# Scaled weights kept in DRAM, a growing lead in the output projection, and another order of z around attention

## The chip, the cores and the metric

The kernel runs on one core of one Trainium2 chip. The metric is the device time of one execution in microseconds (us), smaller is better. TensorE is called PE here, VectorE DVE, ScalarE ACT, GpSimd POOL, and SyncE, which only issues DMAs in this kernel, SP.

## The reference

A decoder trunk of two layers works on 1024 tokens of width 1024 in float32. Layer 0 is a gated MLP with a spatial mixing in chunks of 128 tokens, then one shared pair of keys and values is made, and layer 1 is sliding-window attention:

```python
u, v, z = split(rms_norm(h, a_pre) @ w_in, 3)            # 2048 wide each
v = layer_norm(gelu(v), ln_g, ln_b)
s = einsum('gts,bnsgc->bntgc', tril(w_s), chunks(v)) + b_s
h = h + rms_norm((gelu(u) * s * silu(z)) @ w_out, a_post)
k, v = rms_norm(h, kv_norm) @ w_k, rms_norm(h, kv_norm) @ w_v   # shared, 4 heads of 64
q, z = split(rms_norm(h, b_pre) @ b_in, 2)               # 1024 wide each
o = attention(q, k, v)          # 16 heads, window 128, ALiBi, sinks
h = h + rms_norm((o * silu(z)) @ b_out, b_post)
```

## The kernel before, in words

**Products.** The kernel keeps float32 accuracy by splitting every operand into a high part (made by ACT, L105) and a low part (made by DVE, L106), and by taking three matmuls for one product (`mm3`, L168 to L170): high by high, high by low, low by high. Nearly all of PE's time goes into these, in shapes of 128x128 by 128x512. The large products of layer 0 use a recursive scheme that multiplies sums of blocks.

**Halves.** The 1024 tokens are two halves of 512 (h = 0, 1). Activations of a half stand transposed, eight pieces of 128 rows by 512 tokens.

**Layer 0.** The v projection begins with its first step written out by hand (L400 to L420): x and the weights r0 are loaded in pieces of 512 columns, ACT scales x, DVE casts the weights (L411) and makes both low parts (L412, L414). After u, z and the spatial mixing, the gated products are stored to DRAM as `td`, seven sets m = 1 to 7 by eight groups. Four sets of each group are differences made by POOL (`sums`, L616, by the helper line L205) and stored by SP one after the other (L617).

**Output projection** (`out_layer`, L761). Its 28 steps (m, u) each need a piece of `td` (`t_prep`, loaded by SP into `oraw` P2a, then split) and a piece of weights, mostly a sum of two loaded blocks (`s_sum`, loaded into `oraw` P2b and other places, then split by `s_prep`). `prep(n)` prepares step n and makes the sum of step n + 3 (`LEAD = 3`); the sums of steps 0 to 2 stand ahead of the first `prep`. The order in which these are written sets the order of SP's loads.

**Layer 1.** `Weights` (L112) hands out the weight tiles of layer 1, 128x1024 float32 each, in a fixed order: q and kv and z of the first half, then kv, q and z of the second. SP loads a tile two ahead into one of three buffers (`raw_w`). For a q or z tile POOL multiplies its eight blocks of 128 columns by eight gains, one for each partition and block (L140, eight instructions), in both halves anew. Then ACT and DVE split it. A q or z tile is used in eight products of three matmuls, 24 in all, and handed to the queue in four parts, called steps here. The k and v weights take 16 steps for a half, and are split with the gain in the split itself (L109, L110).

**Attention** runs in units, 16 for each half. A unit makes its scores (L1015, L1021) for four heads, DVE and ACT turn them into probabilities, PE transposes these (L1050) into `pt`, ACT copies them (`pc`, L1053), POOL masks the copy in place (L1054), DVE masks another copy (`pp`, L1057), and PE takes eight values matmuls (`o`, L1068 and L1071). `attn` writes the scores of unit i, the values of unit i - 2 and the transposes of unit i - 1 together, and behind them as many filling steps as the schedule gives: `total` steps are spread over 36 places in attention 0, over 30 in attention 1.

**Order.** At the bottom (L1168 to L1196) stands the schedule: the q phase of half 0 beside the residual sum of layer 0 (`chain_a`, which squares and sums rows on ACT, L182, and takes the reciprocal root on POOL, L178), then kv, then z tiles and attention. Each engine has its own queue in program order; a scheduler places the instructions into it. ACT's queue also takes DMA issues.

Of the kernel before, what the change touches and what calls it, by code (L numbers as in the profile page):

```python
# [14 lines left out]
P = 128  # L15
# [35 lines left out]
def tile_yoco(  # L51
# [56 lines left out]
    def split_scaled(hi, lo, src, g):  # L108
        nc.scalar.activation(hi, src, AF.Copy, scale=g)  # L109
        nc.vector.scalar_tensor_tensor(lo, src, g, hi.bitcast(F32), ALU.mult, ALU.subtract)  # L110

    class Weights:  # L112


        def __init__(self):
            self.order = []
            q, z = ([(wqz[i, m], "q") for m in range(8)] for i in range(2))
            kv = [(wkv[kp], f"kv{kp}") for kp in range(4)]
            self.order += q + kv + z + kv + q + z
            self.order += [(wo_b[gd, cp], "") for gd in range(2) for cp in range(4)]  # L120
            self.raw, self.done, self.at = [], [], 0

        def load(self, i):
            while len(self.raw) <= min(i, len(self.order) - 1):
                n = len(self.raw)
                src, kind = self.order[n]
                self.raw.append(wload(src, f"w{n}"))

        def split(self, i):
            while len(self.done) <= min(i, len(self.order) - 1):  # L130
                n = len(self.done)
                self.load(n)
                raw, kind = self.raw[n], self.order[n][1]
                hi = wpool.tile([P, 1024], F32R, tag="whi", name=f"whi{n}")
                lo = wpool.tile([P, 1024], F32R, tag="wlo", name=f"wlo{n}")
                halves = [slice(kk * 512, kk * 512 + 512) for kk in range(2)]
                if kind == "q":
                    rv = raw.rearrange("p (k c) -> p k c", k=KT)
                    for k in range(KT):
                        nc.gpsimd.tensor_scalar(rv[:, k], rv[:, k], gain(G_BPRE, k), None, ALU.mult)  # L140
                if kind[:2] == "kv":
                    for kk, cs in enumerate(halves):
                        split_scaled(hi[:, cs], lo[:, cs], raw[:, cs], gain(G_KV, 2 * int(kind[2:]) + kk))
                else:
                    split(hi, lo, raw)
                self.done.append((hi, lo))

# [140 lines left out]
    def v_layer(ahead):  # L288
# [119 lines left out]
        for k in range(2):  # L408
            cs = slice(k * 512, k * 512 + 512)
            nc.scalar.activation(T[1][0][:, k], xa[:, 0, k], AF.Copy, scale=g(0, k))  # L410
            nc.vector.tensor_copy(p0[0][:, cs], r0[:, cs])  # L411
            nc.vector.scalar_tensor_tensor(T[1][1][:, k], xa[:, 0, k], g(0, k), T[1][0][:, k].bitcast(F32),  # L412
# [348 lines left out]
    def out_layer():  # L761
# [61 lines left out]

        def prep(n):
            if n < len(steps):
                ready[n] = (t_prep(*steps[n]), s_prep(*steps[n]))
            if n + LEAD < len(steps):
                s_sum(*steps[n + LEAD])

        LEAD = 3  # L830
        yo = [None, None]
# [361 lines left out]

    fill = chain(z_phase(1, n1, z1, 2, 8), tail())
    attn(1, q1, z1, fill, 56, 2)
    drain(fill)  # L1196
# [61 lines left out]
```

## Time and profile before

| what | value |
|---|---|
| runs | 1062.0, 1063.74, 1064.31 us (median 1063.74) |
| profiled execution, its own time | 1062.32 us |
| its span | 1060.6 us, 14401 instructions |
| granted clock of PE | 0.999 |
| DVE, ACT, POOL busy | 71%, 55%, 34% |
| DMA | 159.76 MB, mean 151 GB/s; HBM read 127.37 MB, written 31.46 MB |

The span is what the profile shows from the first to the last instruction; the execution's own time has some 1.7 us around it. A row of the timeline gives the start, the duration of one or a run of instructions, the engine, the line of the program, the operation and its operands, and in brackets how long the engine was idle before it and what ended that. Matmuls are pipelined, so the step from one start to the next is what a matmul costs, not its printed duration. The list of waits gives total, number and longest in us.

### The profile page before, as it was taken

How to read it: one execution, taken by the hardware profiler on the slowest of the kernel's cores; microseconds unless marked ns; L12 is line 12 of the kernel's file. 1: busy time of each engine (PE TensorE's matmuls, PEld its weight loads, DVE VectorE, ACT ScalarE, POOL GpSimd, SP SyncE). 2: the span in 40 equal slices, each digit the busy share in tenths (PEclk: the TensorE clock that was granted, in tenths of full speed). 3: DMA queues.
4: the chain of work that ended last, by engine and by line, in shares of the span. 5: the costliest groups of instructions: out<-in, count | busy, mean ns of one | idle time of the engine just before them, and what ended most of it. 6: DMA issues, size and time to landing. Idle time of an engine off the chain costs nothing.

```text
span 1060.6 us, 14401 instructions
## 1 busy us (share of the span) xinstructions
PE 1045.6 (99%) x5114; PEld 856.6 (81%) x5114; DVE 757.9 (71%) x1353; ACT 581.3 (55%) x981; POOL 357.2 (34%) x407
## 2 busy tenths in 40 slices
PE   9999999999999999999999999999999999999997
PEld 7887788888888888888788888888778778777776
DVE  7987466867767768668696686655767874777873
ACT  6684454555564555464444564545785555765631
POOL 0000003254253442540100354648617779400120
PEclk9999999999999999999999999999999999999999
DMA  8787252434333423348987533734211212112353
GB/s 314 264 284 255 97 180 89 133 110 135 115 109 125 143 105 130 115 142 285 337 304 268 195 140 95 258 100 145 94 60 61 80 60 80 60 60 80 120 179 119
DMA packets 68710, 159.76 MB, mean 151 GB/s; under 512 B 6176, under 2 KB 16800, under 8 KB 68640
## 3 DMA queue, kind: packets, MB, share of 16 engines
q1 hardware_dynamic: 63600, 150.11, 41.7%
q10 hardware_dynamic: 5040, 8.75, 2.3%
q8 instruction: 40, 0.66, 0.3%
q14 instruction: 30, 0.25, 0.1%
HBM read 127.37 MB, written 31.46 MB: 150 GB/s over the span
## 4 chain that ended last, share of the span: by engine, by line
PE 83%; DVE 5%; issue 5%; POOL 3%; DMA 2%; ACT 1%; SPq 0%; DVEq 0%; POOLq 0%; ACTq 0%
PE ob L168 5%; PE ob L170 5%; PE ob L169 5%; PE ub L168 5%; PE ub L170 5%; PE ub L169 5%; PE qz L168 5%; PE qz L169 5%; PE qz L170 5%; PE uc L168 2%; PE uc L170 2%; PE uc L169 2%; PE sp L596 2%; PE vb L169 2%; PE vb L170 2%
## 5 line engine op out<-in xcount | busy, mean ns | idle before, releaser
L140 POOL TENSOR_SCALAR raw_w<-raw_w,gn 128x128 f32<-128x128 f32 x256 | 183.8, 736 | 160.0 <-DVE ohiloP0b L106 93.5
L168 PE MATMUL qz<-n_hi,whi 128*128 128x512 f32 x256 | 102.2, 399 | 0.1
L170 PE MATMUL qz<-n_hi,wlo 128*128 128x512 f32 x256 | 100.2, 391 | 0.0
L169 PE MATMUL qz<-n_lo,whi 128*128 128x512 f32 x256 | 100.0, 390 | 0.0
L106 DVE TENSOR_TENSOR wlo<-raw_w,whi 128x1024 fp32r<-128x1024 f32 x40 | 49.5, 1238 | 37.7 <-ACT whi L105 34.7
L1054 POOL TENSOR_SCALAR_AFFINE_SELECT pc<-pc 128x512 f32<-128x512 f32 x32 | 25.3, 791 | 119.2 <-ACT pc L1053 119.2
L105 ACT ACTIVATE whi<-raw_w 128x1024 fp32r<-128x1024 f32 x40 | 42.2, 1055 | 40.6 <-PE qz L169 14.2
L205 POOL TENSOR_TENSOR f<-raw_uz 128x512 f32<-128x512 f32 x15 | 19.4, 1291 | 130.0 <-DMA bsb<-in_bs_dram 85.7
L205 POOL TENSOR_TENSOR f<-raw_uz,raw_uz 128x512 f32<-128x512 f32 x15 | 19.2, 1280 | 124.9 <-DVE uzhilo_g L106 124.9
L105 ACT ACTIVATE uzhilo_g<-f 128x1024 fp32r<-128x1024 f32 x31 | 32.9, 1060 | 47.7 <-PE uc L170 42.5
L170 PEld LDWEIGHTS qz<-n_hi,wlo 128*128 128x128 f32 x256 | 48.1, 188 | 10.8 <-DVE wlo L106 0.6
L168 PEld LDWEIGHTS qz<-n_hi,whi 128*128 128x128 f32 x256 | 48.1, 188 | 10.7 <-ACT whi L105 0.4
L169 PEld LDWEIGHTS qz<-n_lo,whi 128*128 128x128 f32 x256 | 48.2, 188 | 9.3
L208 ACT ACTIVATE uz_slots<-ub 128x512 f32<-128x512 f32 x48 | 28.4, 591 | 43.6 <-PE ub L170 41.3
L106 DVE TENSOR_TENSOR uzhilo_g<-f,uzhilo_g 128x1024 fp32r<-128x1024 f32 x31 | 39.0, 1257 | 18.6 <-ACT uzhilo_g L105 18.6
L1037 ACT ACTIVATE pr<-pr,nm 128x129 f32<-128x129 f32 x128 | 49.8, 391 | 3.9 <-DVE nm L1035 3.8
L168 PE MATMUL ub<-T,whi_g 128*128 128x512 f32 x128 | 50.6, 396 | 0.0
L168 PE MATMUL ub<-T,uzhilo_g 128*128 128x512 f32 x128 | 50.5, 394 | 0.0
L170 PE MATMUL ub<-T,wlo_g 128*128 128x512 f32 x128 | 49.9, 390 | 0.0
L170 PE MATMUL ub<-T,uzhilo_g 128*128 128x512 f32 x128 | 49.9, 390 | 0.0
L169 PE MATMUL ub<-T,whi_g 128*128 128x512 f32 x128 | 49.8, 389 | 0.0
L169 PE MATMUL ub<-T,uzhilo_g 128*128 128x512 f32 x128 | 49.8, 389 | 0.0
(328 smaller groups left out, 3225.3 us busy)
## 6 DMA issues: line engine op xcount, KB each, us to landing
raw_uz<-in_wuz_in_dram SPq DMA_DIRECT2D x32, 512.0 KB, 3.5
raw_w<-in_wqz_dram SPq DMA_DIRECT2D x32, 512.0 KB, 3.5
td<-uz_slots SPq DMA_DIRECT2D x56, 256.0 KB, 2.2
orawP2a<-td SPq DMA_DIRECT2D x28, 512.0 KB, 4.1
raw<-in_wv_in_dram SPq DMA_DIRECT2D x17, 512.0 KB, 5.3
vg<-vd SPq DMA_DIRECT2D x8, 1024.0 KB, 5.4
orawP2b<-in_wo_a_dram SPq DMA_DIRECT2D x16, 512.0 KB, 5.8
vraw<-in_wv_in_dram SPq DMA_DIRECT2D x13, 512.0 KB, 4.7
```

Of the source, the lines that this page charges most:

```text
L105: nc.scalar.activation(hi, src, AF.Copy)
L106: nc.vector.tensor_tensor(lo, src, hi.bitcast(F32), ALU.subtract)
L140: nc.gpsimd.tensor_scalar(rv[:, k], rv[:, k], gain(G_BPRE, k), None, ALU.mult)
L168: nc.tensor.matmul(out, lhsT=a_hi, rhs=b_hi, start=start, stop=False, skip_group_check=True)
L169: nc.tensor.matmul(out, lhsT=a_hi, rhs=b_lo, start=False, stop=False, skip_group_check=True)
L170: nc.tensor.matmul(out, lhsT=a_lo, rhs=b_hi, start=False, stop=stop, skip_group_check=True)
L205: (eng or nc.vector).tensor_tensor(out, a, b, op)
L208: nc.scalar.activation(out, a, AF.Copy)
L596: nc.tensor.matmul(psv[:, n], lhsT=d["vg"][:, 4 * j + n, i * P:(i + 1) * P], rhs=d["wc"], start=True, stop=True)
L1037: nc.scalar.activation(pr[:, i], pr[:, i], AF.Exp, bias=nm[:, i // 2, i % 2:i % 2 + 1], accum_out=dn[:, i // 2, i % 2:i % 2 + 1])
L1054: nc.gpsimd.affine_select(pc, pc, [[0, 4], [1, P]], ALU.is_ge, 0.0, base=0, channel_multiplier=-1)
```

## The change

There are four edits.

1. *Weights.* A q or z tile of the first half is multiplied by one POOL instruction over 128x1024, with the gains broadcast along each block, in place of eight. The scaled tile is then stored to a DRAM tile `wsc` by a DMA that ACT issues (16 stores of 512 KB). The second half loads `wsc`, and POOL scales nothing there.
2. *First v step.* The two casts of r0 (128x512) go from DVE to POOL.
3. *Output projection.* Ahead of `prep(n)` sums are made up to step n + min(3, max(0, n - 4) // 2), so the lead grows from 0 to 3; `prep(0)` and `prep(1)` both stand ahead of the loads of `s_view`.
4. *Schedule.* All eight z tiles of half 0, with the norm of half 1 beside them, precede attention 0. It is filled with kv, q and the first four z tiles of half 1, 64 steps (72 of 80 before, and two z tiles of half 1 alone behind it). Attention 1 is filled with the other four z tiles and the tail, 48 steps (56 before).

```diff
+    wsc = [[dram.tile([P, 1024], F32, name=f"wsc{i}_{m}") for m in range(8)] for i in range(2)]
...
-            q, z = ([(wqz[i, m], "q") for m in range(8)] for i in range(2))
-            kv = [(wkv[kp], f"kv{kp}") for kp in range(4)]
-            self.order += q + kv + z + kv + q + z
+            q, z = ([(wqz[i, m], "q", wsc[i][m]) for m in range(8)] for i in range(2))
+            q1, z1 = ([(wsc[i][m], "", None) for m in range(8)] for i in range(2))
+            kv = [(wkv[kp], f"kv{kp}", None) for kp in range(4)]
+            self.order += q + kv + z + kv + q1 + z1
...
                 if kind == "q":
                     rv = raw.rearrange("p (k c) -> p k c", k=KT)
-                    for k in range(KT):
-                        nc.gpsimd.tensor_scalar(rv[:, k], rv[:, k], gain(G_BPRE, k), None, ALU.mult)
+                    g = gn[:, G_BPRE:G_BPRE + KT].unsqueeze(2).broadcast_to([P, KT, P])
+                    nc.gpsimd.tensor_tensor(rv, rv, g, ALU.mult)
...
                     split(hi, lo, raw)
+                if back is not None:
+                    nc.scalar.dma_start(out=back, in_=raw)
...
-            nc.vector.tensor_copy(p0[0][:, cs], r0[:, cs])
+            nc.gpsimd.tensor_copy(p0[0][:, cs], r0[:, cs])
...
         def prep(n):
+
+            while sums[0] < len(steps) and sums[0] <= n + min(3, max(0, n - 4) // 2):
+                s_sum(*steps[sums[0]])
+                sums[0] += 1
             if n < len(steps):
                 ready[n] = (t_prep(*steps[n]), s_prep(*steps[n]))
-            if n + LEAD < len(steps):
-                s_sum(*steps[n + LEAD])
-
-        LEAD = 3
+
+        sums = [0]
...
-        for n in range(2):
-            s_sum(*steps[n])
-        s_sum(*steps[2])
         prep(0)
+        prep(1)
         for u in range(4):
             fetch(s_view(u), u, 1, 0)
-        prep(1)
...
-    for _ in z_phase(0, n0, z0, 0, 2):
+    for _ in z_phase(0, n0, z0, 0, 8):
         step(side)
+    drain(side)
     q1 = pair("P3", "q1")
-    fill = chain(z_phase(0, n0, z0, 2, 8), side, kv_phase(1, n1), q_phase(1, n1, q1))
-    attn(0, q0, z0, fill, 72)
+    fill = chain(kv_phase(1, n1), q_phase(1, n1, q1), z_phase(1, n1, z1, 0, 4))
+    attn(0, q0, z0, fill, 64)
     drain(fill)
-    drain(z_phase(1, n1, z1, 0, 2))
...
-    fill = chain(z_phase(1, n1, z1, 2, 8), tail())
-    attn(1, q1, z1, fill, 56, 2)
+    fill = chain(z_phase(1, n1, z1, 4, 8), tail())
+    attn(1, q1, z1, fill, 48, 2)
```

Lines of the changed kernel are five or six higher than those of the one before. Three places show how the queues move.

SP's queue at the start of the output projection, before. `td4` to `td7` are stores of POOL's differences, `orawP2a` takes pieces of `td`, `orawP2b` pieces of weights, `gpa` is a gain:

```order
L710 DMA gpa_3835<-in_a_post_dram 128x1024
L236 DMA orawP2b_3841<-in_wo_a_dram 128x2x512
L617 DMA td5_99<-uz_slots_1333 128x512
L617 DMA td6_100<-uz_slots_1333 128x512
L617 DMA td7_101<-uz_slots4_1334 128x512
L617 DMA td4_98<-uz_slots_1333 128x512
L236 DMA orawP2b_3841<-in_wo_a_dram 128x2x512
L236 DMA orawP2a_3840<-td1_95 128x2x512
L236 DMA scho_3837<-in_wo_a_dram 128x2x512 x4
```

The same place in the changed kernel:

```order
L716 DMA gpa_3851<-in_a_post_dram 128x1024
L242 DMA orawP2a_3856<-td1_111 128x2x512
L623 DMA td5_115<-uz_slots_1349 128x512
L623 DMA td6_116<-uz_slots_1349 128x512
L623 DMA td7_117<-uz_slots4_1350 128x512
L623 DMA td4_114<-uz_slots_1349 128x512
L242 DMA orawP2b_3857<-in_wo_a_dram 128x2x512 x2
L242 DMA scho_3853<-in_wo_a_dram 128x2x512 x4
```

The load of `td1` moved from behind the four stores to ahead of them, and one load of weights moved behind them.

ACT's queue at the end of layer 0 (`junk_oa01` are the last sums of squares of the projection, `n0` the normed half 0, `whi` the high parts of q tiles), before:

```order
L105 ACTIVATE whi1_4989<-raw_w1_4857 128x1024
L105 ACTIVATE n0_hi_4588<-nt0_3_0_4913 128x4x128
L105 ACTIVATE n0_hi_4588<-nt0_3_1_4920 128x4x128
L182 ACTIVATE junk_oa01_0_4940,ssa1_3843<-yoa1_2_4289 128x512
L182 ACTIVATE junk_oa01_1_4944,ssa1_3843<-yoa1_2_4289 128x512
L182 ACTIVATE junk_oa01_2_4948,ssa1_3843<-yoa1_3_4290 128x512
L182 ACTIVATE junk_oa01_3_4952,ssa1_3843<-yoa1_3_4290 128x512
L105 ACTIVATE whi2_5049<-raw_w2_4859 128x1024
```

And in the changed kernel:

```order
L105 ACTIVATE whi1_4999<-raw_w1_4873 128x1024
L151 DMA wsc0_3_91<-raw_w3_5005 128x1024
L105 ACTIVATE n0_hi_4604<-nt0_3_0_4929 128x4x128
L105 ACTIVATE n0_hi_4604<-nt0_3_1_4936 128x4x128
L188 ACTIVATE junk_oa01_0_4956,ssa1_3859<-yoa1_2_4305 128x512
L151 DMA wsc0_4_92<-raw_w4_5059 128x1024
L188 ACTIVATE junk_oa01_1_4960,ssa1_3859<-yoa1_2_4305 128x512
L188 ACTIVATE junk_oa01_2_4964,ssa1_3859<-yoa1_3_4306 128x512
L188 ACTIVATE junk_oa01_3_4968,ssa1_3859<-yoa1_3_4306 128x512
L105 ACTIVATE whi2_5053<-raw_w2_4875 128x1024
```

Two stores of scaled tiles now stand among them; each waits for POOL's multiply of its tile.

PE's queue in attention 0, the values of unit 0_1 (`o_0_1`), the transposes (`pt_0_1`) and the filling matmuls behind them, before:

```order
L1068 MATMUL o_0_1_6412<-pc_0_1_6335,vt 64x256
L1071 MATMUL o_0_1_6412<-pp_0_1_6338,vt 64x256
L1068 MATMUL o_0_1_6412<-pc_0_1_6335,vt 64x256
L1071 MATMUL o_0_1_6412<-pp_0_1_6338,vt 64x256
L1050 MATMUL pt_0_1_6421<-ident,pr_0_1_6295 128x128 x4
```

And in the changed kernel, where `qz_0_2` is a filling product:

```order
L1073 MATMUL o_0_1_6468<-pc_0_1_6406,vt 64x256
L174 MATMUL qz_0_2_6435<-n_hi,whi_6349 128x512
L175 MATMUL qz_0_2_6435<-n_lo,whi_6349 128x512
L176 MATMUL qz_0_2_6435<-n_hi,wlo_6350 128x512
L174 MATMUL qz_0_2_6435<-n_hi,whi_6349 128x512
L175 MATMUL qz_0_2_6435<-n_lo,whi_6349 128x512
L176 MATMUL qz_0_2_6435<-n_hi,wlo_6350 128x512
L174 MATMUL qz_0_2_6435<-n_hi,whi_6349 128x512
L175 MATMUL qz_0_2_6435<-n_lo,whi_6349 128x512
L176 MATMUL qz_0_2_6435<-n_hi,wlo_6350 128x512
L174 MATMUL qz_0_2_6435<-n_hi,whi_6349 128x512
L1076 MATMUL o_0_1_6468<-pp_0_1_6409,vt 64x256
```

Ten filling matmuls now stand between the first values matmul and the rest of its group. Over both attentions the queue has four values groups cut like this (two before), one scores group cut (none before), and seven units whose transposes stand apart from their values (three before). The number of matmuls is the same.

More of the change, by code (lines that the diff above doesn't have):

```diff
@@ L116, in __init__ @@
             self.order = []
-            q, z = ([(wqz[i, m], "q") for m in range(8)] for i in range(2))
-            kv = [(wkv[kp], f"kv{kp}") for kp in range(4)]
-            self.order += q + kv + z + kv + q + z
-            self.order += [(wo_b[gd, cp], "") for gd in range(2) for cp in range(4)]
+            q, z = ([(wqz[i, m], "q", wsc[i][m]) for m in range(8)] for i in range(2))
+            q1, z1 = ([(wsc[i][m], "", None) for m in range(8)] for i in range(2))
+            kv = [(wkv[kp], f"kv{kp}", None) for kp in range(4)]
+            self.order += q + kv + z + kv + q1 + z1
+            self.order += [(wo_b[gd, cp], "", None) for gd in range(2) for cp in range(4)]
             self.raw, self.done, self.at = [], [], 0
@@ L125, in load @@
                 n = len(self.raw)
-                src, kind = self.order[n]
+                src, kind, back = self.order[n]
                 self.raw.append(wload(src, f"w{n}"))
@@ L132, in split @@
                 self.load(n)
-                raw, kind = self.raw[n], self.order[n][1]
+                raw, (src, kind, back) = self.raw[n], self.order[n]
                 hi = wpool.tile([P, 1024], F32R, tag="whi", name=f"whi{n}")
```

## The prediction

> **What bounds the kernel now.** I read the engine totals of the page first, then the waits of TensorE (PE), then the windows in which they lie, and last the timeline and the chain at those places.
>
> ```profile
> PE 1045.6 (99%) x5114; PEld 856.6 (81%) x5114; DVE 757.9 (71%) x1353; ACT 581.3 (55%) x981; POOL 357.2 (34%) x407
> ```
>
> PE is busy for 1045.6 us, 99% of the span. The change leaves out no matmul and adds none, so only three things can move the end: the few microseconds in which PE waits, the time PE loses between matmuls of different shapes, and new waits. A faster POOL is worth nothing by itself.
>
> ```profile
> PE o L1068 <- POOL pc L1054: 2.3, 2, 2.1
> PE ob L168 <- ACT ohiloP0a L105: 1.8, 1, 1.8
> ...
> PE vb L168 <- DVE whi_v L411: 0.8, 1, 0.8
> ...
> PE ob L170 <- DVE ohiloP0a L106: 0.5, 1, 0.5
> ```
>
> The columns are total, times and longest. These four rows are the waits that the change reaches: the values matmuls of attention behind POOL's mask (2.3 us), the third step group of the output projection (1.8 + 0.5), and the very first matmul (0.8). Together that is 5.4 us, and no more than that can be won from waits here.
>
> What a matmul costs is read from starts, because durations overlap:
>
> ```profile
> 906.78 0.66 PE L1068 MATMUL o<-pc,vt 128*64 128x256 f32 x4
> ...
> 907.80 0.66 PE L1050 MATMUL pt<-ident,pr 128*128 128x128 f32 x4
> 908.21 0.48 PE L168 MATMUL qz<-n_hi,whi 128*128 128x512 f32 x1
> 908.53 0.39 PE L169 MATMUL qz<-n_lo,whi 128*128 128x512 f32 x1
> 908.76 0.40 PE L170 MATMUL qz<-n_hi,wlo 128*128 128x512 f32 x1
> ```
>
> A projection matmul (128x512) starts 0.23 us after the one before it (908.53 to 908.76), though its row says 0.39. The eight values matmuls of one attention unit take 1.02 us (906.78 to 907.80) when they stand together. The first matmul after the small ones costs 0.32 (908.21 to 908.53), 0.09 more than its 0.23.
>
> **The change part by part.**
>
> *First v step.* The cast of r0 goes from VectorE (DVE) to POOL.
>
> ```profile
> 4.94 0.75 DVE L412 SCALAR_TENSOR_TENSOR T<-xa,gn,T 128x512 fp32r<-128x512 f32 x1 [3.88 <-ACT T L410]
> 5.61 0.42 DVE L411 CAST whi_v<-raw_v 128x512 fp32r<-128x512 f32 x1
> 6.06 0.69 DVE L414 TENSOR_TENSOR wlo_v<-raw_v,whi_v 128x512 fp32r<-128x512 f32 x1
> ```
>
> The cast stood on DVE behind a multiply of 0.75 us, so it began late; PE waited 0.8 us for it. On POOL it begins when its data lands, beside that multiply. Its length there isn't in the trace. The nearest row of POOL is a two-input 128x512 (1.29 us, below), so I bound it by 0.42 and 1.29. At 0.42 the low half follows the multiply at once and 0.4 us are won; at 1.29 the low half comes some 0.3 us later than now. I take −0.25, between the ends but nearer the gain, since the cast has one input. Bounds −0.4 and +0.3.
>
> *Growing lead.* In the output projection the queue of SyncE (SP) had this order:
>
> ```profile
> 503.27 5.28 SPq L617 DMA_DIRECT2D td<-uz_slots  x4
> ...
> 505.31 1.74 DVE L106 TENSOR_TENSOR ohiloP0b<-orawP2b,ohiloP0b 128x1024 fp32r<-128x1024 f32 x1 [3.43 <-ACT ohiloP0b L105]
> 505.93 2.27 POOL L205 TENSOR_TENSOR uz_slots<-uz_slots 128x512 f32<-128x512 f32 x1
> ```
>
> ```profile
> 509.07 6.57 DMA orawP2a<-td
> ```
>
> The first of these rows is four stores, each waiting for one of POOL's four subtractions, the last of which ends at 508.20. Only behind them, at 509.07, was the load of td1's last piece issued, and it landed at 515.64. ACT's split of that piece and then PE waited for it. In the new order that load stands ahead of the four stores, so it goes out near 503.3, 5.8 us earlier. The piece is then there before ACT reaches it, and both waits go: −1.8 − 0.5 = −2.3. What is late next is the piece of td2, whose load is one place earlier in the queue than it was and is not waited for now. The piece of weights (orawP2b) that falls behind the stores in exchange is for a later step. Bounds: −2.8 (the first matmul behind such a wait is also slow) and 0 (another load takes its place).
>
> *Weights scaled once.* In the first half POOL scales each tile by one two-input instruction of 128x1024 instead of eight of 128x128, and ACT's queue issues a store of the scaled tile. In the second half nothing is scaled. Two effects, the gain first:
>
> ```profile
> 830.95 5.61 POOL raw_w L140 x6
> ...
> 843.55 1.34 POOL pc L1054
> ```
>
> ```profile
> 844.93 0.66 PE L1068 MATMUL o<-pc,vt 128*64 128x256 f32 x4 [2.14 <-POOL pc L1054]
> ```
>
> Three q tiles were scaled in a row on POOL from 830.95, and the mask of the attention unit (L1054) came behind them: 2.14 us of idle PE. Without scaling in attention the mask runs as soon as its copy is there, and the wait goes: −2.1. What is late next is DVE, below.
>
> The cost lies in the first half, in the q phase. ACT's store of tile 4 waits for POOL, and three sums of squares stand behind it on ACT (order in the section on the change).
>
> ```profile
> 657.78 5.97 POOL L140 TENSOR_SCALAR raw_w<-raw_w,gn 128x128 f32<-128x128 f32 x8 [0.87 <-DMA raw_w<-in_wqz_dram]
> 663.73 1.03 POOL L178 TENSOR_TENSOR rpa<-rpa,small 128x4 f32<-128x4 f32 x1
> ```
>
> ```profile
> 657.45 0.63 ACT L182 ACTIVATE junk_oa<-yoa 128x512 bf16<-128x512 f32 x1 [1.52 <-DVE yoa L205]
> ...
> 658.21 0.63 ACT L182 ACTIVATE junk_oa<-yoa 128x512 bf16<-128x512 f32 x1
> ...
> 661.26 0.63 ACT L182 ACTIVATE junk_oa<-yoa 128x512 bf16<-128x512 f32 x1 [1.57 <-DVE yoa L205]
> ```
>
> ```profile
> L205 POOL TENSOR_TENSOR f<-raw_uz 128x512 f32<-128x512 f32 x15 | 19.4, 1291 | 130.0 <-DMA bsb<-in_bs_dram 85.7
> ```
>
> The new multiply has the data of two 128x512 two-input instructions (1291 ns each), so 2 x 1.29 = 2.58 us; the eight old ones took 5.97 here. If it takes 2.58, ACT gets on at 657.78 + 2.58 = 660.36. The three squares, 0.76 us apart (657.45 to 658.21), are then through at 660.36 + 3 x 0.76 = 662.64, where now it is 661.26 + 0.76 = 662.02: +0.6. The reciprocal root of POOL (663.73) waited until the scaling ended at 663.75, and can now start when its sum is there, an estimated 0.7 us earlier. The two cancel: 0. At 4.54 us (two at the contended 2.27 above) the hold is 2.0 us longer, at 5.9 it is 3.3. PE has no slack here:
>
> ```profile
> 668.93 0.39 PE L169 MATMUL qz<-n_lo,whi 128*128 128x512 f32 x1
> 669.36 0.51 PE L170 MATMUL qz<-n_hi,wlo 128*128 128x512 f32 x1
> ```
>
> It already starts 0.2 us late at 669.36 behind this chain. I take 0, as the nearest row is the uncontended one, with ends −0.2 and +2.0. The Trainium skill gives a two-input add over 2048 fp32 columns on this engine as 4497 ns ("GPSIMD Engine Reference", section 3), from which I estimate 2.25 us for 1024; by it the sum would be 0.2 better. No row here shows that shape.
>
> *Schedule.* All eight z tiles of the first half now precede attention 0, and in attention the filling steps fall 64 + 48 instead of 72 + 56. The steps themselves are the same. What changes is where the queue of PE cuts an attention unit. A cut unit of before:
>
> ```profile
> 974.07 0.65 PE L1068 MATMUL o<-pc,vt 128*64 128x256 f32 x2
> ...
> 976.78 0.33 PE L1050 MATMUL pt<-ident,pr 128*128 128x128 f32 x1
> ```
>
> Between these rows stand the eight values matmuls and four filling ones: 2.71 − 4 x 0.23 = 1.79 us against 1.02 uncut, so a cut inside the group costs 0.77. The order has two such cuts before and four now: +1.5. It also cuts a scores group once (none before), and parts the transposes from the values seven times instead of three. A return to filling costs 0.09, so four partings are +0.4, and the scores cut, between 0.09 and 0.77, I put at +0.3. Together +2.2, ends 0 and +3.2. The Trainium skill says that a change of tiling mode drains TensorE ("TensorEngine Tiling (Array Packing)", Tiling Modes, Key Properties). It speaks against this change. The rows agree at the values (`128*64` among `128*128`), but transposes share the mode of the fill, so by the rule the four partings would be free and the part +1.8.
>
> *DVE in attention 0.* The units now have less fill between them while their own DVE work stays.
>
> ```profile
> 820.00:840.00 20.00, 20.00 (x111) 15.99 (x110) 18.87 (x54) 12.58 (x31) 13.21 (x19) 1.00 0.25 80
> ```
>
> Columns: length, PE, PE loads, DVE, ACT, POOL. Where kv ends and q begins, DVE is busy for 18.87 of 20 us. With 64 steps for 72 that stretch is about a tenth tighter, and some of it must show: +0.5, ends 0 and +4.
>
> **The sum.** −0.25 − 2.3 − 2.1 + 0 + 2.2 + 0.5 = −1.95 us. The profiled execution took 1062.32 us, so 1060.4. That run lies 1.4 us under the median of the runs shown (1063.74), from which the sum gives 1061.8. I forecast 1061.0, between the two.
>
> **The rivals.**
>
> *A, cuts that don't hurt* (1058). The cuts cost little because PE would have waited at those places anyway, and DVE keeps up. Then −0.25 − 2.3 − 2.1 = −4.7 remains; 1062.32 − 4.7 = 1057.6. For it: only two cut units are there to price. Against it: both cost the same, and neither waited at the cut itself.
>
> *B, the multiply is slow* (1066, the other side). If POOL needs 4.5 us for it, beside DVE or because the gain is read again for each column, ACT's queue stops at the stores. At tile 4 that costs 2.0. In the order the same pattern stands twice more, ahead of a q scaling and ahead of the first copy of kh; at the same price all three give 6.0, so 1061.0 + 6.0 = 1067.0, and 1065.0 if one of them is hidden: 1066. It decides from where three holds reach the 4.9 us up to 1065.9, at 2.58 + 4.9 / 3 = 4.2 us for the multiply. For it: 505.93 shows 2.27 for an instruction that takes 1.29 alone. Against it: 1.29 is the mean over fifteen. The Trainium skill says that POOL and VectorE share their way to SBUF, and contend when DVE has two SBUF inputs ("GPSIMD Engine Reference", section 1). The trace agrees: at 505.31 DVE's subtraction beside it took 1.74.
>
> *C, DVE becomes the bound in attention 0* (1064.5). With DVE at 94% in 820 to 840 already, each later unit waits for its scores and probabilities; at +4 in place of +0.5 the time is 1061 + 3.5. Against it: only one 20 us window is that full.
>
> *D, no gain at the output projection* (1063). The early load lands late or the split is held up behind another piece on ACT; then +2.3 on the forecast.
>
> **How the numbers follow.** About 0.2% (2.1 us) is what a measurement of this kernel can tell from no change. From 1063.74 that is a line at 1061.6 and one at 1065.9. Forecast 0.47: its terms spread it from 1058 to 1063.5, half of it faster (0.23), nearly all the rest no change (0.22), slower 0.02. A 0.20, all faster. B 0.15: slower 0.11, same 0.04. C 0.12: slower 0.06, same 0.06. D 0.06: same 0.05, slower 0.01. In all faster 0.43, same 0.37, slower 0.20. The range takes in A from 1057 and B and C up to 1066.5; outside it lie the ends of A and B, less than 0.2.
>
> **What would show each step.** Right: no wait of o for pc over 0.3 us; no wait of ob for ohiloP0a near 515; vb's first wait under 0.6; the multiply's row at 2.2 to 2.9 us; values groups cut four times at 0.7 to 0.8 each. Wrong: a multiply over 4.2 us, with PE waits behind q_hi, kh or rpa (B); PE waits for DVE's pr or pp in attention 0 (C); an ohiloP0a wait that stays (D); cut units no longer than uncut ones (A).

## The result, and the profile after

The changed kernel is slower: 1069.65 us in the median of 6 runs (1067.93 to 1072.44), against 1063.48 for the kernel before (6 runs, 1061.32 to 1065.12). The ratio is 1.0056, 95% interval 1.0045 to 1.0068. The forecast was 1061.0 with a range up to 1066.5. The profiled execution took 1069.82 us with a span of 1068.1. Executions of one kernel differ with the clock that PE was granted: those of the kernel before span 1059.5 to 1061.9 us where its mean is 0.999, and 1062.3 to 1064.6 where it is 0.996.

From the page of the changed kernel, the engine totals and the group of the one multiply:

```profile
PE 1050.6 (98%) x5114; PEld 857.8 (80%) x5114; DVE 762.0 (71%) x1351; ACT 569.1 (53%) x973; POOL 206.9 (19%) x169
...
L144 POOL TENSOR_TENSOR raw_w<-raw_w,gn 128x1024 f32<-128x1024 f32 x16 | 33.6, 2101 | 193.0 <-DMA raw_w<-in_wqz_dram 167.8
```

POOL lost 150 us of work and PE the same 5114 matmuls need 5 us more of busy time: the starts lie further apart. The waits of PE in the changed kernel:

```profile
PE oc L174 <- DVE yoa L211: 3.1, 2, 2.6
PE qz L176 <- DVE wlo L106: 1.6, 2, 1.0
PE o L1076 <- DVE pp L1062: 1.5, 2, 0.8
PE nt L761 <- DVE hb L755: 1.2, 1, 1.2
```

The waits of before for POOL's mask and for `ohiloP0a` are gone, as forecast. Others have come, and every one of these four is a wait for DVE.

To see where the time is, I split both executions at the same points of the program. Attention is counted without its fill: from the first scores to the first matmul behind the last values, less 0.2273 us (the step of a 128x512 matmul) for each filling matmul of that size, half for one of 256 columns. The rows at its ends, of before:

```profile
740.39 0.30 PE L1015 MATMUL s<-kh,q_hi 128*128 128x128 f32 x1
...
1021.36 0.50 PE L168 MATMUL ob<-wob_hi,q_hi 128*128 128x512 f32 x1
```

and of the changed kernel:

```profile
776.48 0.22 PE L1020 MATMUL s<-kh,q_hi 128*128 128x128 f32 x1
...
1028.54 0.50 PE L174 MATMUL ob<-wob_hi,q_hi 128*128 128x512 f32 x1
```

Before has fill worth 864 matmuls there, the changed kernel 720. So it is 280.97 − 864 x 0.2273 = 84.6 us before and 252.06 − 720 x 0.2273 = 88.4 after. The same reckoning for the runs that matter below (one profiled execution each, us):

| stretch | before | changed | lead alone (e3) | e4 | e8 | e17 |
|---|---|---|---|---|---|---|
| first ob to first oc (start of the output projection) | 24.60 | 21.76 | 21.76 | 21.76 | 21.76 | 21.76 |
| first oc to first k and v matmul | 178.70 | 183.93 | 179.17 | 180.54 | 179.03 | 183.88 |
| attention without its fill | 84.58 | 88.40 | 84.65 | 88.37 | 82.78 | 83.28 |

The changed kernel wins 2.8 us at the start of the output projection, loses 5.2 between there and the first k and v matmul, and loses 3.8 in attention. Another 0.3 goes ahead of the projection, and 0.7 between k and v and attention. Together 0.3 − 2.8 + 5.2 + 0.7 + 3.8 = 7.2 of the 7.5 us between the two spans.

### The profile page after: what moved, and what is told of

Its sections match the earlier page's. It is cut to its first block, busy times and chain, and to the rows that moved or that the text cites. A ratio compares the mean times of both kernels' runs of the same rounds, so it can differ in the third digit from the quotient of the medians.

```text
span 1068.1 us, 14164 instructions
## 1 busy us (share of the span) xinstructions
PE 1050.6 (98%) x5114; PEld 857.8 (80%) x5114; DVE 762.0 (71%) x1351; ACT 569.1 (53%) x973; POOL 206.9 (19%) x169
## 4 chain that ended last, share of the span: by engine, by line
PE 86%; DVE 6%; DMA 3%; ACT 2%; issue 1%; POOL 1%; SPq 0%; ACTq 0%; DVEq 0%; POOLq 0%
PE ub L174 5%; PE ob L174 5%; PE ub L176 5%; PE ub L175 5%; PE ob L176 5%; PE ob L175 5%; PE qz L174 4%; PE qz L175 4%; PE qz L176 4%; PE uc L174 3%; PE uc L175 3%; PE uc L176 3%; PE sp L602 3%; PE vb L175 2%; PE vb L176 2%; PE vb L174 2%
## 5 line engine op out<-in xcount | busy, mean ns | idle before, releaser
L144 POOL TENSOR_TENSOR raw_w<-raw_w,gn 128x1024 f32<-128x1024 f32 x16 | 33.6, 2101 | 193.0 <-DMA raw_w<-in_wqz_dram 167.8
L174 PE MATMUL uc<-T,uzhilo_g 128*128 128x512 f32 x124 | 48.9, 395 | 0.0
L175 PE MATMUL uc<-T,uzhilo_g 128*128 128x512 f32 x124 | 48.3, 389 | 0.0
```

The lines of the kernel that those rows point to most:

```text
L144: nc.gpsimd.tensor_tensor(rv, rv, g, ALU.mult)
L174: nc.tensor.matmul(out, lhsT=a_hi, rhs=b_hi, start=start, stop=False, skip_group_check=True)
L175: nc.tensor.matmul(out, lhsT=a_hi, rhs=b_lo, start=False, stop=False, skip_group_check=True)
```

## The experiments

Each ratio is against the kernel before, run on the same chip, with its 95% interval.

**The edits alone.** e1 is the kernel before with the schedule edit, e2 with the weights edit, e3 with the growing lead; their diffs are those pieces of the diff above.

> The kernel before with the fourth edit (schedule) alone. Theory 1, read from the two traces (each edit has its own cost): the stretch from the first scores to the last values is about 4 us longer by itself, 1.6 of it from two more cut values groups, 0.3 from parted transposes, the rest from new waits behind DVE; and the waits for POOL's mask stay, since POOL still scales in attention. So 1.003 to 1.006 times the time before, nothing changed ahead of the first z tile. Theory 2 (the weights edit is the whole loss, the schedule is neutral): 0.999 to 1.001.

> The kernel before with the first edit (one multiply, stores of the scaled tiles, loads of them in the second half) alone. Theory 1: the q phase is 2 us longer (44.0 to 46.1) because ACT's queue stands at the stores, the norm of half 1 waits 0.6 longer, the DVE instruction beside POOL's multiply late in the output projection takes 2.9 instead of 1.2, and attention wins the 2.3 us of the waits for POOL's mask less one more cut (0.8): about +1, 1.000 to 1.003. Theory 2 (the scaling in attention was the main loss, the stores are hidden): 0.997 to 0.998.

> The kernel before with the third edit (growing lead) alone. Theory 1: the wait near 515 goes (2.8 us earlier there), and about 1 us of it is lost again near 629, where PE comes to a DVE chain that begins only 0.9 us earlier; no DVE instruction is stretched to 2.9: first norm transposes 1.5 to 2 us earlier, 0.998 to 0.9985. Theory 2 (the end of the output projection is set by something that doesn't move at all, so the whole gain is given back whatever POOL does): first norm transposes at 634.0 as before, 1.000.

Measured: e1 1072.1 us, 1.0077 (1.0063 to 1.0091); e2 1068.8 us, 1.0047 (1.0031 to 1.0062); e3 1061.02 us, 0.9969 (0.9957 to 0.9981). The lead kept its whole gain: 21.76 in the first stretch and only 0.5 lost in the second, where I had expected to lose about 1. Both other edits lose by themselves, each more than expected. In e1 attention without its fill took 94.4 us, against 84.6 before; the first waits of PE were

```profile
PE o L1068 <- POOL pc L1054: 4.4, 3, 2.7
PE ob L168 <- ACT ohiloP0a L105: 1.5, 1, 1.5
PE o L1071 <- DVE pp L1057: 1.2, 1, 1.2
```

so with POOL still scaling there the schedule doubles the wait for the mask. The three ratios add to 0.93% and the changed kernel lost 0.56%: with the schedule, the weights edit takes some of its loss back in attention (94.4 against 88.4). With the old schedule it did not. In e2 attention without its fill took 87.6 us, 3.0 more than before, where I had expected a gain. PE waits 1.9 us there, at 763.28, for the probabilities of a unit, and in front of them a tiny DVE instruction, which takes 0.16 us elsewhere, stood still beside POOL's multiply:

```profile
755.98 2.95 POOL L144 TENSOR_TENSOR raw_w<-raw_w,gn 128x1024 f32<-128x1024 f32 x1 [9.30 <-DMA raw_w<-in_wqz_dram]
```

```profile
757.09 1.87 DVE L1041 TENSOR_SCALAR nm<-mx 128x4 f32<-128x4 f32 x1
```

Another 1.7 us of the 3.0 are a halved clock behind that wait (last section), and one more cut values group is in them too. e2's profiled execution took 1071.29 us, the longest of its six.

**What the weights edit costs in the first half.** Two places in the changed kernel, around the third quadrant of the projection. ACT's queue held by a store, with the multiply in front of it:

```profile
605.10 2.52 POOL L144 TENSOR_TENSOR raw_w<-raw_w,gn 128x1024 f32<-128x1024 f32 x1 [3.17 <-DVE ohiloP0a L106]
```

```profile
607.65 0.33 ACTq L151 DMA_DIRECT2D wsc<-raw_w  x1
608.02 0.60 ACT L188 ACTIVATE junk_oa<-ob 128x512 bf16<-128x512 f32 x1 [3.60 <-PE ob L176]
```

The sum of squares at 608.02 had its data 2 us earlier: in e8, where ACT issues no store, the same row stands at 605.79. And DVE held by the multiply itself:

```profile
627.27 1.90 POOL L144 TENSOR_TENSOR raw_w<-raw_w,gn 128x1024 f32<-128x1024 f32 x1 [3.57 <-DMA raw_w<-in_wqz_dram]
627.34 2.92 DVE L106 TENSOR_TENSOR ohiloP0a<-orawP2a,ohiloP0a 128x1024 fp32r<-128x1024 f32 x1
...
632.13 0.47 PE L174 MATMUL oc<-ohiloP0b,ohiloP0a 128*128 128x512 f32 x1 [2.58 <-DVE yoa L211]
```

POOL began 0.07 us ahead of DVE, and DVE's subtraction took 2.92 instead of 1.22. The chain for which PE then waits 2.58 us is later by these 1.70 and by the store. To part the two, e4 issues the stores from POOL's queue, e5 does that and brings the eight multiplies back:

```diff
-                    nc.scalar.dma_start(out=back, in_=raw)
+                    nc.gpsimd.dma_start(out=back, in_=raw)
```

> The changed kernel with the stores of the scaled tiles issued by POOL, behind the multiply on its own queue, instead of by ACT. Theory 1 (ACT's queue standing at the stores costs the q phase 2 us): q phase back from 46.1 to 44.0 to 44.5 us, so 1.0035 to 1.004 times the time before. Theory 2 (the q phase is late because the multiply holds up DVE, or because the stores take bandwidth from the loads): q phase stays near 46, 1.0055.

> The changed kernel with the stores issued by POOL (as in the run before this) and the old eight multiplies of 128x128 in place of the one of 128x1024. Theory 1 (the one two-input multiply and DVE's instructions hold each other up: 2.92 for 1.22 at 627.34, and 3.59 for 2.1 in the q phase with the stores on POOL): DVE's rows keep their length, the wait of 1.1 near 667 and the one of 0.55 near 629 go to under 0.3 each, 1.5 to 2 us less than with the one multiply. Theory 2 (eight instructions need 5 to 8 us and only move the delay to POOL's own queue): no better, or up to 2 us worse.

e7 and e8 are the same pair without the schedule and cast edits (lead and kept weights on the old order):

> The kernel before with the growing lead and the kept scaled weights, but with the old eight multiplies, the stores issued by POOL, the old schedule and the old cast. Theory 1: the lead's 2.9 and the 2.2 of the wait for POOL's mask add up, less 0.5 for the norm of half 1: 0.995 to 0.9965 times the time before. Theory 2 (the mask's wait turns into one for DVE at the same place): the lead's gain alone, 0.997.

> The kernel of the run before this with the one multiply of 128x1024 instead of eight. Theory 1 (the one multiply and DVE hold each other up): 2 to 5 us slower than that run, with stretched DVE rows beside the multiply near 630, in the q phase and in attention 0. Theory 2 (its length matters, not its kind: 1.9 us instead of 5 to 8): as fast or 1 us faster.

Measured: e4 1067.75 us, 1.0038 (1.0025 to 1.0051); e5 1070.11, 1.0064 (1.005 to 1.0078); e7 1063.2, 1.0005 (0.9994 to 1.0016); e8 1061.15, 0.9977 (0.9968 to 0.9987). So the stores on ACT cost: the second stretch of e4 was 3.4 us shorter. That is clear of its spread: in the six profiles that leave this part of the changed kernel as it is (its own, e6, e9, e13, e17, e18) the stretch takes 182.9 to 183.9 us, in the three with the stores on POOL (e4, e10, e14) 180.4 to 180.5. The gain lies at the end of the output projection (first oc to first q matmul 135.6 us against 137.8) and not in the q phase, where Theory 1 had put it: e4's 44.9 us there lie within the 44.2 to 46.4 of the same six.

Two things are left over in e4. Its second stretch is still 1.4 us longer than with the lead alone, and POOL still holds DVE up:

```profile
624.81 2.11 POOL L144 TENSOR_TENSOR raw_w<-raw_w,gn 128x1024 f32<-128x1024 f32 x1 [3.37 <-DMA raw_w<-in_wqz_dram]
```

```profile
625.08 2.92 DVE L106 TENSOR_TENSOR ohiloP0a<-orawP2a,ohiloP0a 128x1024 fp32r<-128x1024 f32 x1
```

And between k and v and attention e4 takes 74.20 us, the changed kernel 71.95: PE waits 1.9 us for the norm of half 1 instead of 1.2, and the clock is halved for 3.4 us behind that wait (0.57 in the window 738 to 742). So of the 3.4 us won 1.9 are left in the median.

My theory that the one multiply is worse than eight fell, twice: eight are 2 us slower. In e7 DVE's rows kept their length, but POOL's own queue was late:

```profile
607.61 6.14 POOL L144 TENSOR_SCALAR raw_w<-raw_w,gn 128x128 f32<-128x128 f32 x8
614.06 0.60 POOL L151 DMA_DIRECT2D wsc<-raw_w  x1 [0.31 <-POOL raw_w L144]
614.68 1.07 POOL L184 TENSOR_TENSOR rpa<-rpa,small 128x4 f32<-128x4 f32 x1
```

The reciprocal root `rpa`, for which DVE and then PE wait, comes at 614.68; with the lead alone it was at 612.29. e8 shows at the very place of 627.34 what decides between POOL and DVE:

```profile
625.14 1.21 DVE L106 TENSOR_TENSOR ohiloP0a<-orawP2a,ohiloP0a 128x1024 fp32r<-128x1024 f32 x1
...
625.34 3.91 POOL L144 TENSOR_TENSOR raw_w<-raw_w,gn 128x1024 f32<-128x1024 f32 x1 [3.84 <-DMA raw_w<-in_wqz_dram]
```

Here DVE began first, kept its 1.21, and POOL took 3.91 for its 1.90. Between these large instructions, whichever begins first has its way; which one does hangs on a few tenths of a microsecond, so that e8 was spared the 1.70 is luck. The Trainium skill says just this of the two engines ("SBUF — State Buffer", Summary: rules for kernel authors): a DVE instruction with two SBUF inputs and a POOL instruction that reads SBUF exclude each other, and the later one waits until the first has finished. By that rule the multiply costs DVE up to its length, 1.9 us, and the 1.70 here agree. The small multiplies of e7 don't all follow it (last section). I had cited a weaker statement of it and not this one.

**Cuts in attention.** e6 exchanges the two matmuls of each pair of values, so that the first of them needs `pp`, and no group is cut any more:

```diff
+                if b > 0:
+                    nc.tensor.matmul(o[rw, 0:256], lhsT=vt[:, b - 1, vs],
+                                     rhs=self.pp[:, gs].rearrange("p a b -> p (a b)"), start=True, stop=False)
                 nc.tensor.matmul(o[rw, 0:256], lhsT=vt[:, b, vs],
-                                 rhs=self.pc[:, gs].rearrange("p a b -> p (a b)"), start=True, stop=b == 0)
-                if b > 0:
-                    nc.tensor.matmul(o[rw, 0:256], lhsT=vt[:, b - 1, vs],
-                                     rhs=self.pp[:, gs].rearrange("p a b -> p (a b)"), start=False, stop=True)
+                                 rhs=self.pc[:, gs].rearrange("p a b -> p (a b)"), start=b == 0, stop=True)
```

> The changed kernel with the two values matmuls of each pair exchanged (the one on pp first), so that the queue of PE cuts no values group (none instead of four; the scores cut stays). Theory 1 (each cut costs 0.8, and the waits for pp inside a cut group come with it): attention 1.6 to 2.5 us shorter. Theory 2 (PE would wait there anyway, the cut only fills the wait): attention as long as before the exchange, within 0.5.

Measured: 1067.44 us, 1.0037 (1.0022 to 1.0051); attention without its fill 86.6 against 88.4, so 1.8 less, within the range of Theory 1. One of the four cuts, in the changed kernel:

```profile
827.77 0.65 PE L1073 MATMUL o<-pc,vt 128*64 128x256 f32 x2
...
831.86 0.50 PE L175 MATMUL qz<-n_lo,whi 128*128 128x512 f32 x1
```

Between these rows stand eight values matmuls and ten filling ones: 4.09 − 10 x 0.2273 = 1.82 us against 1.02 uncut, so the cut costs 0.80. e6 wins less than four times that; PE's waits for `pp` grew from 1.5 to 2.4 us. e10 joins it with the stores on POOL:

> The changed kernel with both repairs, stores on POOL and the pp matmul first. Theory 1 (the two losses are separate): both gains add, attention without its fill 86.3, the stretch from the second quadrant of the output projection to the first k and v matmul at most 180.5 us (183.9 in the changed kernel), 1.001 to 1.0025. Theory 2 (one hides the other): 1.0035 to 1.004 as each alone.

Measured: 1065.94 us, 1.0015 (1.0005 to 1.0025), 86.6 us and 180.4 us in the two stretches. The two losses are separate and add.

**What else attention loses.** The kept weights save what was forecast (82.3 us in e7, 82.8 in e8, against 84.6). Under the new schedule the same weights give 88.4, 5.6 us more than e8, and the cuts of values groups are 1.8 of them. In the rest are the cut scores group and waits such as these of the changed kernel:

```profile
839.70 0.43 PE L1076 MATMUL o<-pp,vt 128*64 128x256 f32 x1 [0.77 <-DVE pp L1062]
```

```profile
868.27 0.43 PE L1076 MATMUL o<-pp,vt 128*64 128x256 f32 x1 [0.72 <-DVE pp L1062]
```

Three theories in turn. First, that DVE's queue stood at the low parts of the fill; e9 gives these to POOL for the kept tiles:

```diff
+                elif 28 <= n < 44:
+                    nc.scalar.activation(hi, raw, AF.Copy)
+                    nc.gpsimd.tensor_tensor(lo, raw, hi.bitcast(F32), ALU.subtract)
                 else:
                     split(hi, lo, raw)
```

> The changed kernel with the low parts of the second half's sixteen q and z tiles (the subtraction of 128x1024 behind each load of a kept tile) made by POOL instead of DVE; cuts as in the changed kernel. Theory 1 (in attention DVE isn't full, 16 to 17.7 of 20 us, but its queue stands at these subtractions, for which the data isn't there, while pp of the next values group could run): the waits of 0.9 near 838 and 1.1 near 867 go, attention without its fill falls from 88.4 to 86 or 87 us, 1.003 to 1.005 times the time before. Theory 2 (what is lost there is cuts alone, or DVE loses as much to POOL's two-input instruction as it gains): 88 to 89, 1.0055.

Measured: 1069.27 us, 1.0043 (1.0027 to 1.0058), 88.1 us. The waits stayed, and DVE was idle before `pp`:

```profile
836.58 0.18 DVE L1051 RECIPROCAL dn<-dn 128x4 f32<-128x4 f32 x1 [3.32 <-ACT pr L1045]
836.79 1.21 DVE L1052 TENSOR_TENSOR pr<-pr,dn 128x512 f32<-128x512 f32 x1
...
839.14 0.69 DVE L1065 TENSOR_TENSOR pp<-pt,mprev 128x512 f32<-128x512 f32 x1
```

Second, then, that `pp` stands behind that reciprocal for no reason of its own. e13 makes it on POOL from ACT's copy:

```diff
-            nc.gpsimd.affine_select(pc, pc, [[0, 4], [1, P]], ALU.is_ge, 0.0, base=0, channel_multiplier=-1)
             if self.b > 0:
-                self.pp = bp.tile([P, 4, P], F32, tag="pp", name=f"pp{self.id}")
-                nc.vector.tensor_tensor(self.pp, ptv, mprev.unsqueeze(1).broadcast_to([P, 4, P]), ALU.mult)
+                self.pp = pp = bp.tile([P, 4, P], F32, tag="pp", name=f"pp{self.id}")
+                nc.gpsimd.affine_select(pp, pc, [[0, 4], [-1, P]], ALU.is_ge, 0.0, base=-1, channel_multiplier=1)
+            nc.gpsimd.affine_select(pc, pc, [[0, 4], [1, P]], ALU.is_ge, 0.0, base=0, channel_multiplier=-1)
```

> The changed kernel with pp, the second masked copy of the transposed probabilities, made by POOL from ACT's copy (an affine select of 128x512) instead of by DVE from the transposes; the queue of PE then has no cut values group, one scores cut, and one parted transpose. Theory 1 (pp stands on DVE's queue behind a reciprocal that waits for ACT, so the values wait although pp's data is there): the waits for pp go, attention without its fill falls from 88.4 to 84 or 85 us, 3.5 to 4.5 us less than the changed kernel, 1.0015 to 1.0025 times the time before. Theory 2 (only the cuts count, the waits come back at pc or at POOL): as with the pp matmul first, 86.3, 1.0037.

Measured: 1069.55 us, 1.0057 (1.0045 to 1.007), 88.6 us. That theory fell too: the cuts are gone and the waits are now at the mask, many small ones.

```profile
PE o L1073 <- POOL pc L1062: 4.5, 8, 1.2
```

Third, that the gaps are too short. By the order of PE's queue, 12, 18 or 24 filling matmuls stand between the units at the places of attention 0 that wait, where before has 24 or 36. e17 puts two z tiles of half 0 back into attention 0, e18 four:

```diff
-    for _ in z_phase(0, n0, z0, 0, 8):
+    for _ in z_phase(0, n0, z0, 0, 6):
...
-    fill = chain(kv_phase(1, n1), q_phase(1, n1, q1), z_phase(1, n1, z1, 0, 4))
-    attn(0, q0, z0, fill, 64)
+    fill = chain(z_phase(0, n0, z0, 6, 8), kv_phase(1, n1), q_phase(1, n1, q1), z_phase(1, n1, z1, 0, 4))
+    attn(0, q0, z0, fill, 72)
```

> The changed kernel with six z tiles of half 0 ahead of attention 0 instead of eight, the other two as fill inside it (72 steps instead of 64): at least 24 filling matmuls between units in attention 0, one cut values group there instead of three, no scores cut; attention 1 as in the changed kernel. Theory 3 (a unit's chain through DVE, ACT and POOL takes longer than the short gaps, and PE waits for the rest): the waits in attention 0 near 809, 838 and 867 go, attention without its fill falls from 88.4 to 84 to 85.5 us, 1.002 to 1.003 times the time before. Theory 4 (the gaps don't matter, the loss is in the order of q and kv against the units): 87 or more, 1.005.

> The same with four z tiles ahead and four as fill (80 steps): 24 to 48 filling matmuls between units in attention 0, no cut there. Theory 3: nothing more to win than with six ahead but the last cut (0.8), 83.5 to 85 us, unless POOL's multiply in attention 0 holds DVE up (1 to 2 us at one place each). Theory 4: as the changed kernel, 87 or more.

Measured: e17 1064.45 us, 1.0 (0.9989 to 1.0012), 83.3 us; e18 1063.35 us, 1.0 (0.999 to 1.001), 82.9 us. So the place of the z tiles is the cause: two tiles more of fill take 5.1 of the 5.6 us away, waits and cuts together. That it works through the shortest gap, as Theory 3 has it, is argued and not shown. Attention 1 of the changed kernel has gaps of 18 filling matmuls too, and its PE never waits for `pp` or the mask there; and e17 also moves k, v and q to later units. In e17 PE's waits for `pp` are gone. The longest left in its list, apart from the start, lie ahead of attention:

```profile
PE oc L174 <- DVE yoa L211: 2.8, 2, 1.9
PE qz L176 <- DVE wlo L106: 2.2, 2, 1.2
PE nt L761 <- DVE hb L755: 1.4, 1, 1.4
```

**Other versions.** e11 has the lead and the one multiply in both halves with nothing kept (the diff's lines of the multiply without the store), e12 that with the exchange of e6.

> The kernel before with the growing lead and the one multiply of 128x1024 in both halves, with nothing stored or kept, the old schedule and cast. Theory 1 (of the kept weights only the shorter time of POOL in attention counts): the wait for POOL's mask falls from 2.1 to under 0.5, the norm of half 1 waits 0.8 as before and not 2.2, 0.995 to 0.9965. Theory 2 (POOL's multiply in attention takes it back from DVE, up to 1.7 at a place): as the lead alone, 0.997, or worse.

> The kernel of the run before this with the pp matmul first, one cut values group instead of two. Theory 1 (0.8 for a cut): 0.5 to 1 us less than without it. Theory 2 (a wait for pp at the group's head takes its place): no difference.

Measured: e11 1066.95 us, 1.0027 (1.0011 to 1.0043); e12 1067.75, 1.003 (1.0013 to 1.0047). Theory 2 of e11 holds: POOL's multiply in attention holds DVE up, and attention without its fill is 89.3 us. In e11 the first wait of PE is

```profile
PE pt L1049 <- DVE pr L1043: 3.3, 3, 1.9
```

and the longest, at 857.54, stands behind a DVE instruction of 128x4 that took 1.70 us beside a multiply (853.01). e12 tells nothing of the cut, since these waits cover it. e14 to e16 try `pp` on POOL elsewhere:

> The changed kernel with pp on POOL, the pp matmul first and the stores on POOL. Theory 1 (separate losses): 1.8 us less than with pp on POOL alone, 0.9995 to 1.001 times the time before. Theory 2 (the stores on POOL delay its two masks): no better than with pp on POOL alone.

> Growing lead, kept weights with the one multiply and the stores on POOL, old schedule and old cast, and pp on POOL: no cut values group (two before). Theory 1 (the old schedule loses 1.6 to its two cuts and little to DVE's queue): attention without its fill falls from 82.8 to 81 us, 0.996 times the time before. Theory 2 (POOL's multiplies in attention 0 now delay both masks): 82.8 or more, 0.998.

> The kernel before with the growing lead and pp on POOL, scaling still in eight instructions in both halves. Theory 1: the cuts' 1.6 is won, but the wait for POOL's masks grows, as both now stand behind the scaling: attention without its fill 83 to 86 us against 84.6, 0.996 to 0.998. Theory 2 (POOL is free enough): 82.5, 0.995.

Measured: e14 1072.62 us, 1.0085 (1.0071 to 1.0099); e15 1063.59, 1.0003 (0.9994 to 1.0012); e16 1079.21, 1.0149 (1.0135 to 1.0163). None of my gains came from the masks on POOL. In e16 both masks stand behind the scaling, and PE waits 16 us for them where I had allowed for one or two. In e14 attention without its fill takes 93.2 us, with waits now inside the groups: the pair's order and `pp` on POOL seem to work against each other, which no run shows by itself. What the stores do there this run doesn't tell.

Two versions beat both kernels: the lead alone (e3, 0.9969) and the lead with kept weights, stores on POOL and the old order (e8, 0.9977). The second wins 1.9 us more in attention, and gives 1.5 back where the norm of half 1 waits 2.2 us for its load instead of 0.7.

## Why the prediction was wrong

- **First v step, −0.25.** About nothing: the changed kernel comes to the output projection 0.3 us later than before, others with the cast on POOL 0.1 to 0.6 later, those without it between −0.2 and 0.6. It was small, as said; no run has this edit alone, so its sign stays open.
- **Growing lead, −2.3 with −2.8 as an end.** Right, at the end of the range: 24.60 to 21.76 us in every run that has it. That the next thing late would not be waited for holds for the edit alone (e3). In the changed kernel PE comes to the same DVE chain 2.8 us earlier, and the stores and multiplies have made that chain later.
- **Mask without scaling, −2.1.** Right: 84.6 to 82.3 in e7, 82.8 in e8. In e2 the wait for the mask went too, but attention lost it again to a wait behind a multiply that still stands there, a halved clock and a cut.
- **Stores and multiply in the first half, 0 with ends −0.2 and +2.0.** This step failed. It cost 4.8 us (183.93 against the 179.17 of the lead alone): 3.4 are the stores on ACT's queue, as e4 shows, and 1.4 are left with them on POOL, where DVE's subtraction is still held up. I priced one store, that of tile 4, by the multiply's length. The multiply was quicker than I took it (1.90 alone, not 2.58), and the store still cost, because ACT's queue has such stores at other places (607.65). And I let the multiply compete with DVE only in its own duration and not in DVE's. Rival B had the place and the sign, but a slow multiply for its cause, and that was wrong.
- **Cuts, +2.2.** Right for a cut values group. It cost 0.80 in the rows at 827.77, where I had 0.77. The cut scores group was under-priced at +0.3. Its two pieces, from 808.58 to 810.35 and from 813.28 to 813.60, take 2.09 us against 0.99 whole, so 1.1 more, 0.45 of it waiting for DVE. e6 doesn't measure the +2.2 itself: it removes all four values cuts, where I had priced two more, and wins 1.8.
- **DVE in attention, +0.5 with +4 as an end.** This step failed in size and in cause. Beside the values cuts attention lost about 4 us, the cut scores group among them, and DVE was not full: 16.3 of 20 us in the window 820 to 840 of the changed kernel, in which PE waits, and 18.0 in 980 to 1000, in which it doesn't. With more fill between the units of attention 0 the loss went (e17). I had seen that the gaps become shorter by a tenth, and priced the mean gap. That the shortest gap decides is the likeliest reading; why gaps of 18 matmuls are enough in attention 1 stays open.
- **The sum.** With e6's 1.8 for the cuts and the rest of attention as what is left, 0.3 − 2.8 − 2.2 + 5.2 + 0.7 + 1.8 + 4.2 = 7.2 us, against −1.95. The gains are as forecast; the two terms set at 0 and 0.5 make 9.0, and 0.7 came where the norm of half 1 waits for its load beside the stores, for which I had no term.
- **Of the rivals** C (DVE bound) comes nearest in place and price for attention, though DVE was not the bound, and B in the first half; both losses came at once, and the range left no room for that.

## What to carry to other kernels

When a kernel is bound by one engine, a filler moved out of a latency-bound stretch is not free: price the gaps that are left one by one, not by their mean. A DMA that waits for another engine makes every later instruction of the queue that issues it inherit the wait; here it cost less on the queue of the engine that produces its data, though PE then waited longer for the next thing late. Price a POOL instruction also by what it does to DVE beside it.

## What the hardware showed that was not expected

**A wait of PE can be paid twice.** In e16 PE stood still from 835.9 to 842.8 us. The windows (length, PE, loads, DVE, ACT, POOL, granted clock):

```profile
834.00:842.00 8.00, 1.92 (x14) 1.51 (x12) 4.47 (x15) 3.56 (x11) 8.00 (x13) 0.75 0.00 0
842.00:848.00 6.00, 5.16 (x18) 3.56 (x19) 2.13 (x5) 2.00 (x8) 1.12 (x3) 0.50 0.08 12
848.00:854.00 6.00, 6.00 (x35) 4.74 (x34) 1.45 (x3) 2.19 (x6) 3.82 (x8) 0.98 0.23 78
```

The clock had halved during the wait (0.75 in the first window) and stayed at half through the second, over five microseconds behind the wait, so almost 3 us more were lost. Shorter waits did the same in some executions. In e2, around the wait of 1.9 us that ends at 763.28:

```profile
762.00:766.00 4.00, 2.72 (x11) 2.25 (x12) 4.00 (x13) 3.95 (x6) 0.76 (x2) 0.83 0.28 28
766.00:770.00 4.00, 4.00 (x15) 3.24 (x14) 0.56 (x5) 3.03 (x10) 0.47 (x1) 0.75 0.65 241
```

These are 2 x (4 x 0.17 + 4 x 0.25) = 3.4 us at half clock, 1.7 us lost. As much follows the wait of 2.7 us in e1 and that of 1.9 in e4. But the wait of 2.1 us in the kernel before left the clock at 1.00, and so did that of 2.58 at 632.13 in the changed kernel, while in e18 the same wait at the same place was followed by 0.72 in the window 632 to 638. So in these runs the length of a wait alone doesn't decide. The Trainium skill gives a window of about 3.4 us without work after which the clock halves, and as long again with work until it returns ("TensorE: Matmul & The Clock Gate", Part 1, What's actually happening). The trace agrees with the 3.4 us at half clock, and differs in the wait: 1.9 us were enough in e2 and e4.

**POOL's eight small multiplies hardly slow DVE, the one large one does.** Beside the eight in e7 DVE's subtractions of 128x1024 took 1.22 to 1.40 us, and the eight gave way (6.14 us in the row above, and up to 8.55 at another place, where eight at their median of 0.60 would take 4.8); beside the one, DVE's row went from 1.22 to 2.92. A small one gave way even where it began first. In e7

```profile
627.62 1.74 POOL L144 TENSOR_SCALAR raw_w<-raw_w,gn 128x128 f32<-128x128 f32 x1 [3.52 <-DMA raw_w<-in_wqz_dram]
```

```profile
627.74 1.22 DVE L106 TENSOR_TENSOR ohiloP0a<-orawP2a,ohiloP0a 128x1024 fp32r<-128x1024 f32 x1
```

POOL is 0.12 us ahead by the profile and takes 1.74 us, while DVE keeps its 1.22. So the start that the profile shows doesn't always tell which of the two waits.
